# The last four blocks of each MLP written out as one list of single steps, and a raw buffer of its own for one down weight

## The chip, the cores and the metric

The kernel runs on one core of one Trainium2 chip. The time is the device time of one execution in microseconds (us); smaller is better. Below, the engines are called by the names of the profile: PE (TensorE, matrix products and transposes), ACT (ScalarE), DVE (VectorE), POOL (GpSimd) and SP (SyncE, whose queue issues the transfers; "SPq" in a timeline is the issue of one).

## The reference

The program is a small decoder trunk on 512 tokens of width 1024, in fp32: one layer with a pooling mixer, then one layer of stick-breaking attention (16 heads of 64), each followed by an MLP with a squared ReLU. Every mixer and MLP is framed by two RMS norms. Keys and values are projected once, from the residual stream after the first layer. Cut to what matters here:

```python
def sq_relu_mlp(h, w_up, w_down):
    u = jnp.matmul(h, w_up)                          # 512 x 4096
    return jnp.matmul(jnp.square(jax.nn.relu(u)), w_down)

for layer in range(2):
    h = rms_norm(x, mix_pre_g[layer])
    m = pool_mixer(h, ...) if layer < 1 else (stick_breaking_attention(...) @ w_o)
    x = x + rms_norm(m, mix_post_g[layer])
    h = rms_norm(x, mlp_pre_g[layer])
    x = x + rms_norm(sq_relu_mlp(h, w_up[layer], w_down[layer]), mlp_post_g[layer])
    if layer == 0:
        kv = rms_norm(x, kv_norm_g) @ w_kv
```

## The kernel before

**Tiling.** The 512 tokens are T = 4 tiles of 128; the residual stream is kept in `xt[0..3]`, each 128 tokens by 1024. The 4096 hidden units of an MLP are 32 blocks of 128. Each fp32 product is made of three products of a high and a low part (`mm3`, L284 to L286: high by high, high by low, low by high), so every weight and every activation is first split: the high part is a cast on ACT, the low part a subtract on DVE. For a weight this is `weight` (L142): a transfer into a tile "raw", of which there are two buffers (L144), the cast (L154) and the subtract (L156).

**An MLP** (`mlp`, from L604) works on a block of hidden units at a time: the up product (`up_block`, L705 to L707), ReLU (L619), square (L620), split. The down products of blocks 0 to 27 run in five groups, each as a scheme of seven products of half size (class `Seven`: products L587, sums into y on DVE L596, splits L265 and L266). The last four blocks, 28 to 31 (`plain` to `NJ`), are plain products: their down weights ("dn" in the rows) go through `weight`, their places come from `dn_pool`, and `contract` (L426) multiplies. In the last group `fill` (one new weight for each call, if there is a place for it) starts their loads.

**The finish of a tile** follows in `contract`. For each token tile, in two halves of 512 columns (in three cuts of 512, 256 and 256 for the last tile of the last layer): the products of four blocks on PE; `evacuate` on DVE, which adds the sums to y (L449); the sum of squares on ACT (L269); the product with the gain on DVE (L316); then `first_rstd`: the total on POOL (L273, for the three cuts L328) and the power to -1/2 (L280); `add_part` on DVE, which adds the normed result to x (L333). In layer 0 the squares of the new x follow (L269), a second total and power, the scale (`norm_part`, L371, ACT), eight transposes on PE (L385) and their split into the high part (`high`, L395 or L399 with a gain, ACT) and the low part (`low`, L404 or L408, DVE), which are the operands `xnh` and `xnl` of the next product: key and value (cast of a value L887). In layer 1 each cut is written out by SP (L346).

**What sets the order.** A scheduler orders each engine's instructions by a timeline of its own. Around `contract` only PE is held to the program's order (`manual_schedule(engines={PE})`); ACT, DVE and POOL are ordered by the scheduler. Each engine then works through its list in order. SP's queue is in order too: a transfer that waits for a buffer holds up those behind it.

**Key and value weights ahead.** During MLP 0 `split_apart` splits the weights of key, value and the like ahead of time: loads into tiles "apart" (three buffers), scale, cast and subtract in place, and then SP writes both parts to memory ("kept", L196); `make` (L226) reads them back when they are wanted ("w<-kept").

**MLP 1's beginning.** The attention's last steps end with a norm whose four high part copies (L399), scale (L371) and transposes (L385) lead into MLP 1's first up products; the weights of the first group of seven come by "w<-in_wdn" (L526).

Of the kernel before, what the change touches and what calls it, by code (L numbers as in the profile page):

```python
# [81 lines left out]
]  # L82


R_SCALE, R_MIX_POST0, R_MLP_PRE0, R_MLP_POST0, R_MIX_POST1, R_MLP_POST1 = range(6)

C_MIX_PRE0, C_KV, C_MIX_PRE1, C_MLP_PRE1 = range(4)
# [3 lines left out]
def trunk(ctx, tc, x, consts, grow, pw, wup, wdn, wq, wk, wv, wo, out):  # L91
    nc = tc.nc
# [46 lines left out]
    behind, latest = {}, {}  # L139


    def weight(src, tiles, scaled=None):  # L142
        raw = wts.tile([P, D], F32, tag="raw", bufs=2, name=name("raw"))
        nc.sync.dma_start(raw, src)  # L144

        def later(engine):
            return tc.issue_after(behind[engine].ins) if engine in behind else nullcontext()

        if scaled is not None:
            with later("pool"):  # L150
                scaled(raw)
        hi, lo = tiles
        with later("act"):
            nc.scalar.copy(hi, raw)  # L154
        with later("dve"):
            nc.vector.tensor_tensor(out=lo, in0=raw, in1=hi.bitcast(F32), op=ALU.subtract)  # L156
        return hi, lo
# [8 lines left out]

        return scaled

    gate, queue, made, ahead, dn_pool, att_pool = [False], [], {}, 4, [None], [None]

    def want(key, src, scaled=None):
        queue.append((key, src, scaled))
# [110 lines left out]
    def mm3(dst, ah, al, bh, bl, start, stop):  # L283
        nc.tensor.matmul(dst, ah, bh, start=start, stop=False)  # L284
        nc.tensor.matmul(dst, ah, bl, start=False, stop=False)  # L285
        nc.tensor.matmul(dst, al, bh, start=False, stop=stop)  # L286
# [9 lines left out]
    class Update:  # L296
# [18 lines left out]
            cut = self.cuts[n]  # L315
            nc.vector.tensor_tensor(out=self.scaled[:, cut], in0=y, in1=self.gpost[:, cut], op=ALU.mult)  # L316

        def square(self, n, y):

            self.squares_of(n, y)  # L320
            self.product(n, y)

        def first_rstd(self):
            if len(self.cuts) == 2:
                total(self.st, 0, self.eps)
# [15 lines left out]
        def add(self):  # L341
            self.first_rstd()
            for n, cut in enumerate(self.cuts):
                self.add_part(n)
                if self.final:
                    nc.sync.dma_start(out[TS[self.t], cut], xt[self.t][:, cut])  # L346
                else:
                    self.squares_of_x(n)

        def rstd(self):  # L350
            normed_by[self.t] = self
# [16 lines left out]
        def norm_part(self, n):  # L368
# [8 lines left out]
        def norm(self):  # L377
            for n in NS:
                self.norm_part(n)

        def transposes(self, h):
            pt = ps()
# [40 lines left out]
            if t in pending:  # L423
                pending.pop(t).transpose()

    def contract(lhs, w, y, first, update=None, tiles=range(T), soon=False):  # L426


        last = len(lhs) - 1
        ups = {}  # L430
        for t in tiles:
            up = ups[t] = update(t, y[t]) if update is not None else None
            cuts = up.cuts if up is not None else NS
            pds = [ps()[:, : cut.stop - cut.start] for cut in cuts]

            def product(n, cs):
                for c in cs:
                    (lh, ll), (wh, wl) = lhs[c], w[c]
                    mm3(
                        pds[n], lh[:, TS[t]], ll[:, TS[t]], wh[:, cuts[n]], wl[:, cuts[n]],  # L440
                        c == 0, c == last,
                    )

            def evacuate(n):
                part = y[t][:, cuts[n]]
                if first:
                    nc.scalar.copy(part, pds[n])
                else:
                    nc.vector.tensor_tensor(out=part, in0=pds[n], in1=part, op=ALU.add)  # L449
                if up is not None:  # L450
                    up.square(n, part)

            normed = up is not None and not up.final
            if t == 0:
                product(0, range(last))
                product(1, range(last))
                product(0, [last])
            else:
                product(0, range(last + 1))
            if normed and t == T - 1 and not soon:  # L460
                ups[0].transpose()
            evacuate(0)
            if normed and t > 0:
                ups[t - 1].rstd()
                ups[t - 1].norm()
            if t == 0:
                product(1, [last])
            elif normed and t == T - 1:
                product(1, [0])
                ups[1].transpose()  # L470
                product(1, range(1, last + 1))
            else:
                product(1, range(last + 1))
                if normed and soon and t == 2:
                    ups[0].transpose()
            evacuate(1)
            for n in range(2, len(cuts)):
                product(n, range(last + 1))
                evacuate(n)
            if up is None:  # L480
                fill()
            else:
                up.add()
                if normed and t == T - 2:
                    behind.update(latest)
        if normed:
            ups[T - 1].rstd()
            ups[T - 1].norm()
            for t in (T - 2, T - 1):
                pending[t] = ups[t]  # L490

# [106 lines left out]
    def mlp(l, mp, update):  # L598
# [57 lines left out]
        for g, group in enumerate(groups):  # L656
            coming = groups[g + 1] if g + 1 < len(groups) else None
            if coming:
                coming.squares()
            ups = list(range(firsts[g + 1], firsts[g + 1] + 2 * GROUPS[g + 1]) if coming else range(plain, NJ))  # L660
            if g == 0:
                up(ups.pop(0))
                fill()
            else:
                with tc.issue_after(latest["dve"].ins):
                    while entering:
                        entering.popitem()[1].homogeneous_eps()
            for i in range(7):
                group.product(i, y, written if g == 0 else None)
                if 7 * g + i in steps:  # L670
                    with tc.issue_after(latest["act"].ins), tc.issue_after(latest["dve"].ins):
                        split_apart(mp)
                if ups:
                    up(ups.pop(0))
                if i + 2 < 7:
                    group.make(i + 2)
                    if i + 2 == 4 and coming:
                        coming.load(0)
                    if i + 2 == 6 and coming:
# [11 lines left out]
                fill()  # L691
# [177 lines left out]
    with tc.tile_pool(name="att", bufs=1, reuse_waits="tile") as ap:  # L869
# [222 lines left out]
        def out_proj(u, tiles):  # L1092
            if u not in wos:
                wos[u] = [get(("o", 2 * u + c)) for c in range(2)]
            contract([os[2 * u + c] for c in range(2)], wos[u], y, u == 0, None, tiles)

        def end():

# [187 lines left out]
```

## Time and profile before

| | us |
|---|---|
| median of 3 runs | 956.77 (956.1 to 956.96) |
| span of the profiled execution | 955.0 |
| PE busy | 940.7 (98%) |
| DVE busy | 707.1 (74%) |
| ACT busy | 576.6 (60%) |
| POOL busy | 44.7 (5%) |
| last matmul starts | 946.71 |

The profile shows one execution, whose span of 955.0 us runs from its first to its last instruction; the median of the runs stands 1.8 us above it. Times in a timeline count from the start of the span. A row of a timeline gives start, length (both us), engine, line, operation, output<-input, sizes and, in brackets, how long the engine had been idle before and what ended that. Matmuls overlap, so a row's length is longer than the distance to the next one. A row "xN" holds N instructions in a row, and its length is that of all of them.

### The profile page before, as it was taken

How to read it: one execution, taken by the hardware profiler on the slowest of the kernel's cores; microseconds unless marked ns; L12 is line 12 of the kernel's file. 1: busy time of each engine (PE TensorE's matmuls, PEld its weight loads, DVE VectorE, ACT ScalarE, POOL GpSimd, SP SyncE). 2: the span in 40 equal slices, each digit the busy share in tenths (PEclk: the TensorE clock that was granted, in tenths of full speed). 3: DMA queues.
4: the chain of work that ended last, by engine and by line, in shares of the span. 5: the costliest groups of instructions: out<-in, count | busy, mean ns of one | idle time of the engine just before them, and what ended most of it. 6: DMA issues, size and time to landing. Idle time of an engine off the chain costs nothing.

```text
span 955.0 us, 12510 instructions
## 1 busy us (share of the span) xinstructions
PE 940.7 (98%) x4757; PEld 799.6 (84%) x4758; DVE 707.1 (74%) x810; ACT 576.6 (60%) x1015; POOL 44.7 (5%) x88
## 2 busy tenths in 40 slices
PE   9999999999999999999999999999999999999996
PEld 6998888888888878999899988898888888888885
DVE  5875799988979866476577778874595966957856
ACT  6667979788775646456656554775545544444632
POOL 2300000000000004000000000300000000000002
PEclk9999999999999999999999999999999999999998
DMA  8244969789697750422434271342513233133102
GB/s 307 99 175 151 338 216 359 293 282 343 221 326 266 273 192 2 179 88 88 162 125 171 95 265 45 127 139 68 197 39 129 97 132 110 45 132 110 47 21 88
DMA packets 43261, 156.14 MB, mean 163 GB/s; under 512 B 4289, under 2 KB 4673, under 8 KB 43202
## 3 DMA queue, kind: packets, MB, share of 16 engines
q1 hardware_dynamic: 43202, 155.36, 45.4%
q8 instruction: 37, 0.61, 0.3%
q14 instruction: 22, 0.18, 0.1%
HBM read 121.79 MB, written 33.55 MB: 163 GB/s over the span
## 4 chain that ended last, share of the span: by engine, by line
PE 86%; DVE 4%; ACT 3%; POOL 3%; DMA 2%; issue 1%; SPq 0%; POOLq 0%; DVEq 0%; ACTq 0%
PE ps L587 27%; PE ps L707 15%; PE ps L705 15%; PE ps L706 15%; PE ps L284 2%; PE ps L285 2%; PE ps L286 2%; PE ps L1040 2%; ACT xn L269 2%; PE ps L819 1%; PE ps L1023 1%; POOL stat L273 1%; DVE x L333 1%; PE ps L979 1%; POOL stat L280 1%
## 5 line engine op out<-in xcount | busy, mean ns | idle before, releaser
L587 PE MATMUL ps<-w,a 128*128 128x512 f32 x1176 | 278.6, 389 | 0.0
L707 PE MATMUL ps<-xnh,w 128*128 128x512 f32 (+1 forms) x712 | 261.6, 368 | 0.1
L706 PE MATMUL ps<-xnl,w 128*128 128x512 f32 (+1 forms) x712 | 261.5, 368 | 0.0
L705 PE MATMUL ps<-xnh,w 128*128 128x512 f32 (+1 forms) x712 | 261.2, 368 | 0.0
L587 PEld LDWEIGHTS ps<-w,a 128*128 128x128 f32 x1176 | 220.7, 188 | 45.9 <-DVE w L266 0.2
L707 PEld LDWEIGHTS ps<-xnh,w 128*128 128x128 f32 x712 | 134.2, 188 | 22.4 <-DVE w L840 0.3
L706 PEld LDWEIGHTS ps<-xnl,w 128*128 128x128 f32 x712 | 134.2, 189 | 21.8
L705 PEld LDWEIGHTS ps<-xnh,w 128*128 128x128 f32 x712 | 133.7, 189 | 22.1
L596 DVE TENSOR_TENSOR y<-ps,y 128x512 f32<-128x512 f32 x124 | 84.4, 686 | 42.0 <-PE ps L587 41.8
L156 DVE TENSOR_TENSOR w<-raw,w 128x1024 fp32r<-128x1024 f32 x58 | 70.9, 1222 | 57.7 <-ACT w L154 57.5
L154 ACT CAST w<-raw 128x1024 fp32r<-128x1024 f32 x58 | 61.0, 1051 | 80.5 <-PE ps L707 80.5
L265 ACT CAST a<-r 128x768 fp32r<-128x768 f32 (+1 forms) x60 | 47.6, 794 | 72.4 <-PE ps L587 54.6
L266 DVE TENSOR_TENSOR a<-r,a 128x768 fp32r<-128x768 f32 (+1 forms) x60 | 54.0, 900 | 11.8 <-ACT a L265 11.6
L265 ACT CAST w<-e 128x1536 fp32r<-128x1536 f32 (+1 forms) x30 | 41.8, 1395 | 25.6 <-DVE e L561 16.2
L1004 DVE TENSOR_TENSOR_SCAN e<-u,begin 128x1280 f32<-128x1280 f32 x16 | 45.2, 2822 | 11.3 <-ACT u L988 10.4
L266 DVE TENSOR_TENSOR w<-e,w 128x1536 fp32r<-128x1536 f32 (+1 forms) x30 | 49.4, 1647 | 1.8 <-ACT w L265 1.6
L165 ACT ACTIVATE apart<-apart,eye 128x128 f32<-128x128 f32 (+1 forms) x132 | 43.1, 407 | 0.2 <-DMA apart<-in_wk 0.2
L266 DVE TENSOR_TENSOR w<-w,w 128x1536 fp32r<-128x1536 f32 (+1 forms) x20 | 33.0, 1649 | 8.1 <-ACT w L265 8.1
L619 ACT ACTIVATE r<-ps 128x512 f32<-128x512 f32 x56 | 33.0, 589 | 8.3 <-PE ps L707 8.2
L284 PE MATMUL ps<-w,xnh 128*128 128x256 f32 x128 | 36.6, 286 | 1.4 <-ACT xnh L395 1.4
L266 DVE TENSOR_TENSOR w<-xn,w 128x1536 fp32r<-128x1536 f32 (+1 forms) x20 | 33.0, 1650 | 5.6 <-ACT w L265 5.5
L620 ACT ACTIVATE r<-r 128x512 f32<-128x512 f32 x56 | 35.5, 633 | 1.3
(131 smaller groups left out, 1394.7 us busy)
## 6 DMA issues: line engine op xcount, KB each, us to landing
raw<-in_wup SPq DMA_DIRECT2D x64, 512.0 KB, 3.8
w<-kept SPq DMA_DIRECT2D x60, 512.0 KB, 4.1
kept<-wx SPq DMA_DIRECT2D x30, 512.0 KB, 4.9
w<-in_wdn SPq DMA_DIRECT2D x8, 1536.0 KB, 7.7
kept<-apart SPq DMA_DIRECT2D x24, 512.0 KB, 5.1
xn<-in_wdn SPq DMA_DIRECT2D x8, 1536.0 KB, 8.2
raw<-in_wdn SPq DMA_DIRECT2D x8, 512.0 KB, 3.5
apart<-in_wk SPq DMA_DIRECT2D x7, 512.0 KB, 6.4
```

What stands on the lines that cost most here:

```text
L154: nc.scalar.copy(hi, raw)
L156: nc.vector.tensor_tensor(out=lo, in0=raw, in1=hi.bitcast(F32), op=ALU.subtract)
L165: nc.scalar.mul(c, c, gc[:, lo + k : lo + k + 1])
L265: latest["act"] = nc.scalar.copy(hi, src)
L266: latest["dve"] = nc.vector.tensor_tensor(out=lo, in0=src, in1=hi.bitcast(F32), op=ALU.subtract)
L284: nc.tensor.matmul(dst, ah, bh, start=start, stop=False)
L587: nc.tensor.matmul(bank, a[:, x, q, TS[t]], w[:, z, q], start=start and q == 0 and k == 0, stop=q == self.n - 1 and k == 2, skip_group_che ...
L596: nc.vector.tensor_tensor(out=part, in0=bank, in1=part, op=ALU.add)
L705: nc.tensor.matmul(pu[:, cols], wh[:, k, :], xnh[:, k, cols], start=k == 0, stop=False)
L706: nc.tensor.matmul(pu[:, cols], wh[:, k, :], xnl[:, k, cols], start=False, stop=False)
L707: nc.tensor.matmul(pu[:, cols], wl[:, k, :], xnh[:, k, cols], start=False, stop=k == KC - 1)
L1004: nc.vector.tensor_tensor_scan(out=self.e[:, ::-1], data0=self.u[:, 1:][:, ::-1], data1=begin[:, ::-1], initial=0.0, op0=ALU.mult, op1=ALU ...
```

## The change

1. `MLP_ORDER` lists, for each layer, single steps of the last four blocks. A new function `finish` runs the list, with the order of PE, ACT, DVE and POOL all held to it. The letters: p t n c..., products of tile t, cut n, blocks c; v evacuate; s squares; g product with the gain; V first rstd; a add to x; S squares of x; W second rstd; n norm part; t transposes; h and l high and low part; B marks what later weights may follow. `contract` keeps only the case without an update, which the output projection of the attention uses.
2. `weight` takes an optional `raw` tile. For block 30 (`NJ - 2`), the third of the four, the raw tile is a third buffer of the tag "apart", in place of one of the two "raw" buffers.
3. In the last step of the last group `fill` may start two weights instead of one.

In the program that results, the number of matmuls and of other operations is the same. In layer 0 PE's transposes of tile 0 stand ahead of the products of tile 3's first half, and those of tile 1 ahead of its second half; three matmuls of key and value change places; on ACT the second cast of a value (L887) stands ahead of both squares of the last tile's new x (step S30 and S31). Block 30's load stands in SP's queue behind a "kept<-apart" (the one issued at 319.68 before). In layer 1 its load stands right behind the "w<-in_wdn" issued at 607.03 before; its cast stands on ACT between the last squares (L269) and the four copies of L399 at the beginning of MLP 1, and its subtract on DVE between L1167 and L408.

```diff
+MLP_ORDER = [
+    last_steps("""p00012 p01012 p003 v00 s00 p013 v01 s01 g00 g01 V0 p100123 v10 s10 a00 S00 a01 S01 g10 W0
+    p110123 v11 s11 g11 V1 n00 n01 p200123 v20 s20 a10 S10 a11 S11 g20 W1 p210123 v21 s21 g21 V2 n10 n11
+    t00 t01 h00 h01 p300123 v30 s30 a20 a21 B t10 h10 S20 t11 h11 S21 W2 l00 l01 p310123 v31 s31 V3
+    l10 l11 g30 g31 n20 n21 a30 S30 a31 S31 W3 n30 n31"""),
+    last_steps("""p00012 p01012 p003 v00 s00 p013 v01 s01 g00 g01 V0 p100123 v10 s10 a00 a01 g10
+    p110123 v11 s11 g11 V1 p200123 v20 s20 a10 a11 g20 p210123 v21 s21 g21 V2 p300123 v30 s30 g30
+    p310123 v31 s31 a20 p320123 v32 s32 V3 a21 g31 g32 a30 a31 a32"""),
+]
...
-    def weight(src, tiles, scaled=None):
-        raw = wts.tile([P, D], F32, tag="raw", bufs=2, name=name("raw"))
+    def weight(src, tiles, scaled=None, raw=None):
+        if raw is None:
+            raw = wts.tile([P, D], F32, tag="raw", bufs=2, name=name("raw"))
...
-        made[k] = weight(src, place(k), scaled)
+        made[k] = weight(src, place(k), scaled, dn_raw.pop(k, None))
...
-    def contract(lhs, w, y, first, update=None, tiles=range(T), soon=False):
...
+    def contract(lhs, w, y, first, tiles):
...
+    def finish(l, lhs, w, y, update):
+
+        ups = [update(t, y[t]) for t in range(T)]
+        bank = {}
+
+        def product(t, n, *cs):
+            cut = ups[t].cuts[n]
+            if (t, n) not in bank:
+                bank[t, n] = ps()[:, : cut.stop - cut.start]
+            for c in cs:
+                (lh, ll), (wh, wl) = lhs[c], w[c]
+                mm3(
+                    bank[t, n], lh[:, TS[t]], ll[:, TS[t]], wh[:, cut], wl[:, cut], c == 0, c == len(lhs) - 1
+                )
...
+        on = mybir.EngineType
+        with tc.manual_schedule(engines={on.PE, on.Activation, on.DVE, on.Pool}):
+            for step, which in MLP_ORDER[l]:
+                steps[step](*which)
+        if l == 0:
             for t in (T - 2, T - 1):
                 pending[t] = ups[t]
...
                     c, d = (piece("apart", 1, 3)[:, 0] for _ in range(2))
+                    dn_raw["dn", l, NJ - 2] = mp.tile([P, D], F32, tag="apart", bufs=3, name=name("dn"))
...
-                fill()
+                fill(1 + (coming is None and i == 6))
...
-        with tc.manual_schedule(engines={mybir.EngineType.PE}):
-            contract(squares[1:], w, y, False, lambda t, y: update(t, y, gpost))
+        finish(l, squares[1:], w, y, lambda t, y: update(t, y, gpost))
```

More of the change, by code (lines that the diff above doesn't have):

```diff
@@ L82, with last_steps @@
 ]
+def last_steps(text):
+    return [(w[0], [int(c) for c in w[1:]]) for w in text.split()]
+MLP_ORDER = [
[7 more added lines that the diff above has]
+]
 R_SCALE, R_MIX_POST0, R_MLP_PRE0, R_MLP_POST0, R_MIX_POST1, R_MLP_POST1 = range(6)
@@ L167, in gains @@
         return scaled
-    gate, queue, made, ahead, dn_pool, att_pool = [False], [], {}, 4, [None], [None]
+    gate, queue, made, ahead, dn_pool, att_pool, dn_raw = [False], [], {}, 4, [None], [None], {}
     def want(key, src, scaled=None):
@@ L339, in squares_of_x @@
             square_sum(xt[self.t][:, cut], self.xn[:, cut], self.st, 4 + n)
[L341 to L348, printed above, removed]
         def rstd(self):
@@ L375, in norm_part @@
                 )
-        def norm(self):
-            for n in NS:
-                self.norm_part(n)
         def transposes(self, h):
@@ L424, in need @@
                 pending.pop(t).transpose()
-    def contract(lhs, w, y, first, update=None, tiles=range(T), soon=False):
+    def contract(lhs, w, y, first, tiles):
         last = len(lhs) - 1
-        ups = {}
         for t in tiles:
[L432 to L445, printed above, removed]
+            for n in NS:
+                pd = ps()
+                for c, ((lh, ll), (wh, wl)) in enumerate(zip(lhs, w)):
+                    mm3(pd, lh[:, TS[t]], ll[:, TS[t]], wh[:, n], wl[:, n], c == 0, c == last)
+                part = y[t][:, n]
@@ L446, in evacuate @@
                 if first:
-                    nc.scalar.copy(part, pds[n])
+                    nc.scalar.copy(part, pd)
                 else:
[L449 to L480, printed above, removed]
-                fill()
[L482 to L488, printed above, removed]
+                    nc.vector.tensor_tensor(out=part, in0=pd, in1=part, op=ALU.add)
+            fill()
@@ new lines, in finish, with evacuate, add, transposes @@
+    def finish(l, lhs, w, y, update):
[10 more added lines that the diff above has]
+                )
+        def evacuate(t, n):
+            part = y[t][:, ups[t].cuts[n]]
+            nc.vector.tensor_tensor(out=part, in0=bank.pop((t, n)), in1=part, op=ALU.add)
+        def add(t, n):
+            ups[t].add_part(n)
+            if l == 1:
+                cut = ups[t].cuts[n]
+                nc.sync.dma_start(out[TS[t], cut], xt[t][:, cut])
+        def transposes(t, h):
+            bank["t", t, h] = ups[t].transposes(h)
+        steps = {
+            "p": product, "v": evacuate, "a": add, "t": transposes, "B": lambda: behind.update(latest),
+            "s": lambda t, n: ups[t].squares_of(n, y[t][:, ups[t].cuts[n]]),
+            "g": lambda t, n: ups[t].product(n, y[t][:, ups[t].cuts[n]]),
+            "V": lambda t: ups[t].first_rstd(), "S": lambda t, n: ups[t].squares_of_x(n),
+            "W": lambda t: ups[t].rstd(), "n": lambda t, n: ups[t].norm_part(NS[n]),
+            "h": lambda t, h: ups[t].high(h, bank["t", t, h]), "l": lambda t, h: ups[t].low(h, bank["t", t, h]),
+        }
+        on = mybir.EngineType
[3 more added lines that the diff above has]
+        if l == 0:
@@ L1094, in out_proj @@
                 wos[u] = [get(("o", 2 * u + c)) for c in range(2)]
-            contract([os[2 * u + c] for c in range(2)], wos[u], y, u == 0, None, tiles)
+            contract([os[2 * u + c] for c in range(2)], wos[u], y, u == 0, tiles)
         def end():
```

4 lines of the change are left out of this document (removed).

## The prediction

> **What bounds the kernel now.** I read the page's busy shares first, then the chain of work that ended last, then the waits of TensorE alone, then the timeline around each wait that the change can reach.
>
> ```profile
> span 955.0 us, 12510 instructions
> PE 940.7 (98%) x4757; PEld 799.6 (84%) x4758; DVE 707.1 (74%) x810; ACT 576.6 (60%) x1015; POOL 44.7 (5%) x88
> PE 86%; DVE 4%; ACT 3%; POOL 3%; DMA 2%; issue 1%; SPq 0%; POOLq 0%; DVEq 0%; ACTq 0%
> 925.53 3.63 PE ps L587 x16
> ...
> PE ps L284 <- ACT xnh L395: 1.4, 1, 1.4
> PE ps L285 <- DVE dn L156: 0.8, 1, 0.8
> PE ps L284 <- ACT dn L154: 0.7, 1, 0.7
> ```
>
> TensorE is busy for 98% of the span, and the number of its matmuls stays as it is. One 512 column matmul follows the other every 3.63 / 16 = 0.227 us (fourth line, from the chain). So only two things can move the time: a wait of TensorE, or the stretch after its last matmul, where the chain leaves it. The three last lines (waits of TensorE: total, times, longest, us) name most of what the change can reach: one wait at the handover from MLP 0 to the key and value projection (xnh L395) and two for a down weight ("dn"). A fourth place, the transposes that begin MLP 1, is shown under C. Elsewhere TensorE runs back to back, and an edit there is worth nothing: the freed or added work of the other engines lies beside it.
>
> **The change, part by part.**
>
> A. Block 30's weight in layer 0. Timeline rows (start, length, engine, line, operation):
>
> ```profile
> 319.68 0.32 SPq L196 DMA_DIRECT2D kept<-apart  x1
> 334.54 0.51 SPq L196 DMA_DIRECT2D kept<-apart  x1
> 338.94 1.99 ACT L154 CAST dn<-raw 128x1024 fp32r<-128x1024 f32 x2
> 341.13 1.22 DVE L156 TENSOR_TENSOR dn<-raw,dn 128x1024 fp32r<-128x1024 f32 x1
> 342.38 2.06 SPq L144 DMA_DIRECT2D raw<-in_wdn  x2
> 342.87 1.22 DVE L156 TENSOR_TENSOR dn<-raw,dn 128x1024 fp32r<-128x1024 f32 x1
> 345.91 0.39 PE L286 MATMUL ps<-dn,sq 128*128 128x512 f32 x1
> 345.93 1.05 ACT L154 CAST dn<-raw 128x1024 fp32r<-128x1024 f32 x1 [5.00 <-DMA raw<-in_wdn]
> 347.03 0.50 PE L284 MATMUL ps<-dn,sq 128*128 128x512 f32 x1 [0.73 <-ACT dn L154]
> 348.29 0.50 PE L285 MATMUL ps<-dn,sq 128*128 128x512 f32 x1 [0.76 <-DVE dn L156]
> 348.85 0.40 PE L284 MATMUL ps<-dn,sq 128*128 128x512 f32 x1
> kept<-apart SPq DMA_DIRECT2D x24, 512.0 KB, 5.1
> ```
>
> Blocks 28 and 29 fill the two "raw" buffers. Block 30's load waits until the subtract at 341.13 + 1.22 = 342.35 has freed one, is issued at 342.38 and cast at 345.93, as soon as it has landed (3.55 later); and TensorE, which would have begun it at 345.91 + 0.227 = 346.14, begins at 347.03 (0.89 lost), gets the low part at 348.29 instead of 347.26 (1.03 more) and loses another 0.11 by the matmul at 348.85: 2.03.
>
> With a buffer of its own the load waits only for the write "kept<-apart" issued at 319.68, which empties that slot. By the median of 5.1 it lands at 324.8, the weight 3.55 later, by 328.4, well ahead of the cast, which now follows the two casts that end at 338.94 + 1.99 = 340.93. The subtract follows block 29's, which ends at 342.87 + 1.22 = 344.09, so it ends near 345.3, against a need at 346.14 + 0.227 = 346.37: 1.1 to spare. The two y adds (L596) that it pushes back only have to precede the adds of the finish, after this stage. One new wait comes: the low part goes into the slot that the last "kept<-apart" empties. This write is issued at 334.54 and by the median lands at 339.6; the subtract may start as late as 345.15, so the write would have to take 10.6 to be late. Block 31's load then goes out first at 342.38, lands at 345.9, is cast by 347.0 and subtracted by 348.2. TensorE wants its high part after twelve more matmuls (three of block 30, nine of the second half), at 346.14 + 12 x 0.227 = 348.86, and its low part at 349.09: no wait. Gain 2.03. Bounds: 0 (the late write takes it all) and 2.03 (no more is lost there); I take 2.03, as the spare is far above the median.
>
> B. The handover to key and value in layer 0:
>
> ```profile
> 376.03 0.28 PE L286 MATMUL ps<-w,xnl 128*128 128x256 f32 x1
> 376.98 0.63 ACT L269 ACTIVATE xn<-x 128x512 f32<-128x512 f32 x1 [3.12 <-DVE x L333]
> 377.61 0.35 ACT L887 CAST v<-ps 128x256 fp32r<-128x256 f32 x1
> 378.68 0.30 POOL L273 TENSOR_SCALAR stat<-stat 128x1 f32<-128x1 f32 x1 [2.58 <-ACT xn L269]
> 379.66 1.33 ACT L371 ACTIVATE xn<-x,stat 128x512 f32<-128x512 f32 x2 [1.07 <-POOL stat L280]
> 380.90 1.05 ACT L395 CAST xnh<-ps 128x512 fp32r<-128x512 f32 x2
> 381.51 0.39 PE L284 MATMUL ps<-w,xnh 128*128 128x256 f32 x1 [1.45 <-ACT xnh L395]
> ```
>
> TensorE waits 1.45 for tile 2's high part (380.90), which stands on ScalarE behind tile 3's norm: squares of its x (376.98 and, behind the cast of v, 377.86), their sum on GpSimd 378.68, the scale 379.66. If everything were only shifted by A it would start at 379.48. In the listed order the cast of v (L887) stands ahead of both squares on ScalarE, and needs TensorE's second value product, whose last matmul starts at 376.03 before, hence 374.00 after A and, as three value and key matmuls change places, near 374.1, ending at 374.40. Squares at 374.72 and 375.35, sum 376.25 (0.82 behind the second square, as in the rows), scale 377.24, high part 378.48, TensorE 379.09. That is 2.42 ahead of 381.51: 0.39 beyond A. Ends: 0 (only A's shift) and 1.45 (the whole wait goes); I take 0.39, which is a sum of rows. The transposes of tiles 0 and 1, moved ahead of tile 3's products, and the squares, products and scales that change places cost nothing: TensorE's products of tile 3 cover them.
>
> C. The start of MLP 1. There the load of block 30 now comes first in ScalarE's and VectorE's queues, ahead of tile 2's high parts (L399) and tile 3's scale:
>
> ```profile
> 611.45 0.39 PE L286 MATMUL ps<-w,ohl 128*128 128x512 f32 x1
> 621.85 1.11 ACT L399 ACTIVATE xnh<-ps,eye 128x128 fp32r<-128x128 f32 x4
> 623.79 1.27 PE L385 MATMUL ps<-eye,xn 128*128 128x128 f32 x8 [0.37 <-ACT xn L371]
> w<-in_wdn SPq DMA_DIRECT2D x8, 1536.0 KB, 7.7
> ```
>
> The slot's last reader is the matmul at 611.45, so the load goes out near 611.9. By 3.55 it lands at 615.5; by 7.7, the slowest kind of load near it, at 619.6. At 621.85 it is there, and its cast (1.05 in the row of 345.93, 0.95 to 1.05 from one to the next) goes first. The four copies of L399 start at 622.8, the scale behind them as much later, the transposes at 624.6 to 624.7 instead of 623.79. TensorE has no further wait in MLP 1 that could give this back: plus 0.85 (0.82 to 0.95). The subtract lies beside this on VectorE. In exchange a cast and a subtract disappear from the last group of MLP 1, where they hid behind TensorE: nothing.
>
> D. The end. Rows of the last tile:
>
> ```profile
> 943.63 0.69 DVE L316 TENSOR_TENSOR y<-y,grow 128x512 f32<-128x512 f32 x1 [0.79 <-ACT xn L269]
> 943.71 0.87 POOL L273 TENSOR_SCALAR stat<-stat,eps 128x1 f32<-128x1 f32 x1 [3.52 <-ACT xn L269]
> 945.25 1.42 DVE L333 SCALAR_TENSOR_TENSOR x<-y,stat,x 128x512 f32<-128x512 f32 x2 [0.92 <-POOL stat L280]
> 946.71 0.28 PE L286 MATMUL ps<-dn,sq 128*128 128x256 f32 x1
> 947.51 1.02 DVE L316 TENSOR_TENSOR xn<-y,grow 128x512 f32<-128x512 f32 x2
> 948.45 0.42 DVE L449 TENSOR_TENSOR y<-ps,y 128x256 f32<-128x256 f32 x1
> 949.56 0.19 POOL L328 TENSOR_TENSOR stat<-stat 128x1 f32<-128x1 f32 x1 [0.59 <-ACT xn L269]
> 950.42 1.54 DVE L333 SCALAR_TENSOR_TENSOR x<-xn,stat,x 128x512 f32<-128x512 f32 x3 [1.09 <-POOL stat L280]
> L273 POOL TENSOR_SCALAR stat<-stat x24: 294/300/2186, 5.0 to 622.0; 128x1 f32<-128x1 f32 x24
> L273 POOL TENSOR_SCALAR stat<-stat,eps x8: 375/864/869, 354.1 to 948.6; 128x1 f32<-128x1 f32 x8
> ```
>
> The last products end at 946.71 + 0.28 = 946.99, but the last evacuation (L449) starts only at 948.45: VectorE has the two adds of tile 2 (945.25), two evacuations and two products (947.51) ahead of it. In the list the evacuations of tile 3 stand ahead of tile 2's adds and the products g31 and g32 behind the last evacuation. It can start at 947.02, 1.43 earlier. Its square, the sum L328 and the add at 950.42 follow it by 950.42 - 948.45 = 1.97 before, so the add would start near 949.0: a gain of 1.42. But the products now run on VectorE from 948.0 to 948.85, exactly when GpSimd would take L328 (948.14). The two first rows show what such a neighbour does: tile 2's sum starts 0.08 behind an L316 product and takes 0.87. The two last rows (shortest, median, longest in ns) hold all such sums: those with the operand eps, which are taken beside products, have a median of 864, the others of 300, with 2186 once. Then L328 ends behind the products, near 949.0, its power takes it on, and the add starts at 949.69: a gain of 0.73. Ends 0 and 1.42; I take 0.73, since the row at 943.71, with the same neighbour, shows the hold. From the add to the end of the span nothing changes.
>
> This one the Trainium skill speaks against too: its page "SBUF — State Buffer", section "Who interferes with whom", says that VectorE and GpSimd share a port pair that one of them locks, so that the loser is blocked for the whole instruction. The trace agrees, by 864 against 300; by the page the gain would be 0.73, without it 1.42.
>
> The sum: -2.03 - 0.39 + 0.85 - 0.73 = -2.30, so a span of 955.0 - 2.3 = 952.7. The median of the runs shown, 956.77, stands 1.74 above this span; with the same distance it comes to 954.5. A measurement of this kernel can tell about 0.2%, or 1.9, from no change, so the forecast lies just outside.
>
> **The rivals.**
>
> 1. GpSimd isn't held at the end, because L328 comes a little ahead of the products: -2.30 - 0.69 = -2.99, 953.8. For it speaks the small distance, 0.14; against it the row at 943.71, whose product also began first, by only 0.08.
>
> 2. The layer 0 wait is only replaced. Block 30's subtract needs the last "kept<-apart" to have landed; each us that it lands after 345.15 costs a us. At 346.5, 12.0 instead of 5.1, it takes back 1.35: 955.9, within 0.2%. The same comes if VectorE reaches the subtract later than its rows say. That the change doesn't do what it says, because SyncE's queue still holds the load back until 342, would end at the same place; against it, the two rows of SPq at 319.68 and 334.54 show that the queue moves on in that time.
>
> 3. Slower: ScalarE stands at the start of MLP 1 for a weight that has not landed. Its queue is in order, so tile 2's high parts and tile 3's scale wait behind the cast. Each us of landing after 621.85 costs a us: with -2.30 as a base it ends over 0.2% slower once the load lands after 621.85 + 2.30 + 1.91 = 626.1, 14.2 after its issue. At 627.5 it gives 954.5 + 5.65 = 960.1. For it: this is the only place where a load of the far future is put ahead of work that TensorE waits for at once. Against: 7.7 is the longest median there.
>
> **How the numbers follow.** The forecast with A to D as summed gets 0.47, rival 1 0.15, rival 2 and smaller gains of any kind 0.24, rival 3 and its like 0.14. So faster by over 0.2% has 0.62, within 0.2% 0.24, slower 0.14. Predicted is 954.5. The range goes from 953.4 (the other end of D and 0.4 of what B could still give) to 956.6 (all of A lost and no more): it leaves out most of rival 3 and a little below. The forecast's own range is 953.8 to 955.2.
>
> **What would show it.** A: no wait of TensorE on dn L154 or L156 in layer 0, and the load of block 30 issued between 322 and 325. B: a wait for xnh L395 of some 1.2 instead of 1.45, the first key and value matmul after it near 379.1. C: a cast dn L154 near 621.9 and the transposes 0.85 later relative to the matmul at 611.45. D: L449's last start 0.3 behind the last product, and L328 longer than 0.19. A wait for a DMA on ScalarE at C, a "kept<-apart" landing behind 344 or new waits of TensorE in the finish would prove the forecast wrong.

## The result

The changed kernel takes 954.3 us (median of 7 runs, 953.63 to 954.42), the kernel before 956.77 beside it (956.1 to 957.52). The ratio is 0.9973, with a 95% interval of 0.9962 to 0.9984: faster by about 0.27%. The medians differ by 2.47 us, against 2.30 forecast (954.5). The span of the profiled execution is 951.9 against 955.0. Of these 3.2 us, 0.66 lie ahead of everything that the change touches (the first product with a down weight in layer 0 starts at 340.49 instead of 341.15) and are chance: in the executions below that start lies anywhere from 340.49 to 341.34.

**The profile after.** The page's span, busy shares and chain by engine, then the waits of TensorE (total, times, longest, us). Line numbers have moved: L154 is L170 now, L156 L172, L269 L285, L273 L289, L280 L296, L284 to L286 are L300 to L302, L316 L332, L328 L339, L333 L344, L371 L373, L385 L383, L395 L393, L399 L397, L449 L455.

```profile
span 951.9 us, 12511 instructions
PE 940.5 (99%) x4758; PEld 799.6 (84%) x4758; DVE 707.5 (74%) x810; ACT 576.9 (61%) x1015; POOL 45.5 (5%) x88
PE 93%; ACT 2%; POOL 1%; DVE 1%; issue 1%; DMA 1%; SPq 0%; POOLq 0%; DVEq 0%; ACTq 0%
...
PE ps L383 <- ACT xn L373: 1.3, 2, 1.1
PE ps L300 <- ACT xnh L393: 0.9, 1, 0.9
```

Both waits for "dn" are gone. The wait for xnh has shrunk from 1.4 to 0.9, and the one of the transposes for xn has grown from 0.5 to 1.3. TensorE does the same work (940.5 against 940.7).

A, timeline of layer 0 (start, length, engine, line, operation):

```profile
319.04 0.32 SPq L212 DMA_DIRECT2D kept<-apart  x1
321.66 0.33 SPq L160 DMA_DIRECT2D dn<-in_wdn  x1
340.18 1.05 ACT L170 CAST dn<-dn 128x1024 fp32r<-128x1024 f32 x1
341.72 0.33 SPq L160 DMA_DIRECT2D raw<-in_wdn  x1
343.34 1.22 DVE L172 TENSOR_TENSOR dn<-dn,dn 128x1024 fp32r<-128x1024 f32 x1
345.25 0.39 PE L302 MATMUL ps<-dn,sq 128*128 128x512 f32 x1
345.48 0.39 PE L300 MATMUL ps<-dn,sq 128*128 128x512 f32 x1
345.32 1.05 ACT L170 CAST dn<-raw 128x1024 fp32r<-128x1024 f32 x1 [4.10 <-DMA raw<-in_wdn]
```

Block 30's load (dn<-in_wdn) goes out at 321.66, 20 us ahead of its old place (each taken from the first product with a down weight), its cast and its subtract (343.34, ended 344.56) are done well ahead of the matmul at 345.48, and TensorE goes on in its 0.23 pitch from 345.25. The load at 341.72 is now block 31's.

B, the handover to key and value:

```profile
373.74 0.37 ACT L877 CAST v<-ps 128x256 fp32r<-128x256 f32 x1 [0.57 <-PE ps L302]
374.01 0.64 ACT L285 ACTIVATE xn<-x 128x512 f32<-128x512 f32 x1
375.44 0.30 POOL L289 TENSOR_SCALAR stat<-stat 128x1 f32<-128x1 f32 x1 [2.50 <-ACT xn L285]
376.42 1.33 ACT L373 ACTIVATE xn<-x,stat 128x512 f32<-128x512 f32 x2 [1.07 <-POOL stat L296]
377.66 1.05 ACT L393 CAST xnh<-ps 128x512 fp32r<-128x512 f32 x2
378.28 0.38 PE L300 MATMUL ps<-w,xnh 128*128 128x256 f32 x1 [0.94 <-ACT xnh L393]
```

The cast of v stands ahead of the squares and sets their start, as forecast, and the rest of the chain keeps its old distances.

C, the start of MLP 1:

```profile
608.68 0.33 SPq L160 DMA_DIRECT2D dn<-in_wdn  x1
618.65 1.03 ACT L170 CAST dn<-dn 128x1024 fp32r<-128x1024 f32 x1
619.59 1.12 ACT L397 ACTIVATE xnh<-ps,eye 128x128 fp32r<-128x128 f32 x4
620.60 1.33 ACT L373 ACTIVATE xn<-x,stat 128x512 f32<-128x512 f32 x2
621.37 0.94 PE L383 MATMUL ps<-eye,xn 128*128 128x128 f32 x5 [1.14 <-ACT xn L373]
```

The cast goes first. Counted from tile 2's transposes, it pushes the four copies back by 0.93 against before, and the scale and tile 3's transposes by 0.78 and 0.77; it waits for no transfer (its row has no releaser), since the load left 10 us ahead of it.

D, the end:

```profile
944.60 0.42 DVE L455 TENSOR_TENSOR y<-ps,y 128x256 f32<-128x256 f32 x1 [0.35 <-PE ps L302]
944.94 0.74 DVE L344 SCALAR_TENSOR_TENSOR x<-y,stat,x 128x512 f32<-128x512 f32 x1
945.60 0.75 DVE L332 TENSOR_TENSOR xn<-y,grow 128x256 f32<-128x256 f32 x2
945.72 0.35 POOL L339 TENSOR_TENSOR stat<-stat 128x1 f32<-128x1 f32 x1 [1.05 <-ACT xn L285]
946.14 0.63 POOL L296 TENSOR_TENSOR stat<-stat,mhalf 128x1 f32<-128x1 f32 x1
946.81 0.75 DVE L344 SCALAR_TENSOR_TENSOR x<-xn,stat,x 128x512 f32<-128x512 f32 x1 [0.45 <-POOL stat L296]
```

The last evacuation waits for TensorE alone, 0.32 behind the last matmul's start at 944.28. GpSimd's last sum takes 0.35 beside a product and 0.19 before.

**The span cut in pieces.** To compare executions that start differently, each span is cut at the same instructions: the first and the last matmul with a down weight in layer 0 (A lies between), the matmul that follows tile 2's transposes (B), tile 3's transposes in MLP 1 (C), the last matmul, the last tile's first add (D) and the end. Each piece is the difference of two starts in the trace of that kernel, in us; the kernels below the second are those of the experiments.

| kernel | start | A | B | C | to last matmul | D | add to end | span | SP records |
|---|---|---|---|---|---|---|---|---|---|
| before | 341.15 | 29.02 | 11.34 | 242.28 | 322.92 | 3.71 | 4.61 | 955.03 | 466 |
| changed | 340.49 | 26.95 | 10.84 | 243.09 | 322.91 | 2.53 | 5.04 | 951.85 | 468 |
| changed, again | 341.02 | 27.22 | 10.83 | 243.05 | 322.92 | 2.52 | 5.05 | 952.61 | 468 |
| order only | 341.18 | 29.15 | 10.83 | 242.28 | 322.92 | 2.52 | 4.62 | 953.50 | 466 |
| raw buffer only | 341.34 | 27.32 | 11.34 | 243.05 | 322.91 | 3.71 | 5.05 | 954.72 | 468 |
| raw buffer in layer 0 only | 341.03 | 27.00 | 10.84 | 242.27 | 322.91 | 2.53 | 5.02 | 951.60 | 467 |
| before, one more transfer | 340.83 | 29.01 | 11.37 | 242.28 | 322.93 | 3.72 | 4.99 | 955.13 | 468 |
| layer 0 only, tile 0 out in one | 340.96 | 26.99 | 10.84 | 242.29 | 322.92 | 2.52 | 4.84 | 951.36 | 465 |
| layer 0 only, tiles 0 and 1 out in one each | 341.07 | 26.98 | 10.83 | 242.28 | 322.93 | 2.52 | 4.73 | 951.34 | 463 |
| no product beside the last sum | 341.11 | 27.00 | 10.83 | 243.05 | 322.91 | 2.30 | 5.05 | 952.25 | 468 |
| g30 last | 340.94 | 27.41 | 10.84 | 243.05 | 322.92 | 2.53 | 5.05 | 952.74 | 468 |

From before to changed: A -2.07, B -0.50, C +0.81, D -1.18, the stretch behind the add +0.43. Together -2.51, and the medians differ by 2.47. The columns "add to end" and "SP records" (SyncE's records in the trace) hold what the prediction did not see.

### The profile page after: what moved, and what is told of

It is laid out like the page before. It is cut to its first block, busy times and chain, and to the rows that moved or that the text cites. A ratio compares the mean times of both kernels' runs of the same rounds, so it can differ in the third digit from the quotient of the medians.

```text
span 951.9 us, 12511 instructions
## 1 busy us (share of the span) xinstructions
PE 940.5 (99%) x4758; PEld 799.6 (84%) x4758; DVE 707.5 (74%) x810; ACT 576.9 (61%) x1015; POOL 45.5 (5%) x88
## 4 chain that ended last, share of the span: by engine, by line
PE 93%; ACT 2%; POOL 1%; DVE 1%; issue 1%; DMA 1%; SPq 0%; POOLq 0%; DVEq 0%; ACTq 0%
PE ps L577 28%; PE ps L697 15%; PE ps L695 15%; PE ps L696 15%; PE ps L300 4%; PE ps L302 4%; PE ps L301 4%; PE ps L1030 2%; PE ps L1013 2%; PE ps L809 1%; PE ps L969 1%; ACT xn L285 1%; PE ps L970 1%; PE ps L383 1%; POOL stat L289 1%
## 5 line engine op out<-in xcount | busy, mean ns | idle before, releaser
L172 DVE TENSOR_TENSOR w<-raw,w 128x1024 fp32r<-128x1024 f32 x58 | 70.9, 1222 | 56.7 <-ACT w L170 56.5
L170 ACT CAST w<-raw 128x1024 fp32r<-128x1024 f32 x58 | 61.0, 1051 | 78.0 <-PE ps L697 77.8
L300 PE MATMUL ps<-w,xnh 128*128 128x256 f32 x128 | 36.5, 286 | 0.9 <-ACT xnh L393 0.9
```

## The experiments

**The parts apart.** Three kernels and the changed one again, timed beside the kernel before on one chip. The first keeps the list and drops the raw buffer:

```diff
-                    dn_raw["dn", l, NJ - 2] = mp.tile([P, D], F32, tag="apart", bufs=3, name=name("dn"))
-                fill(1 + (coming is None and i == 6))
+                fill()
```

> The listed order alone; block 30's weight goes through the two shared raw buffers again, in both layers. Theory (the four terms are separate): the layer 0 wait for the weight is back (two waits of TensorE on dn L170 and L172, about 2.0 together), the 0.8 at the start of MLP 1 is gone, B (about -0.5) and D (about -1.2) stay. Sum about -1.7 against before, near 955.1. Rival (the order gains only because the products run without a gap): the wait eats B too, since tile 3's norm chain then stands where it stood, and about -1.2 is left, near 955.6.

Measured: 955.35 against 956.85, ratio 0.9984 (0.9975 to 0.9993). The waits of TensorE in its trace:

```profile
PE ps L300 <- ACT xnh L393: 0.9, 1, 0.9
PE ps L300 <- ACT dn L170: 0.9, 1, 0.9
PE ps L301 <- DVE dn L172: 0.8, 1, 0.8
PE ps L383 <- ACT xn L373: 0.5, 2, 0.4
```

The two waits for dn are back in full, the transposes wait 0.5 as before, and the wait for xnh stays at 0.9. By the pieces A and C are those of before (+0.13, 0.00), B and D those of the changed kernel (-0.51, -1.19): -1.56, measured -1.50. So B is the list's own gain and does not hang on the raw buffer; the rival falls. That it is the place of the cast of v within the list is read from the chain in B; the single swaps of the list were not run apart.

The second is the kernel before with the raw buffer and without the list:

```diff
+        if raw is None:
+            raw = wts.tile([P, D], F32, tag="raw", bufs=2, name=name("raw"))
...
+                    dn_raw["dn", l, NJ - 2] = mp.tile([P, D], F32, tag="apart", bufs=3, name=name("dn"))
...
+                fill(1 + (coming is None and i == 6))
```

> Before, with only the raw buffer of its own and the second load in the last step; ACT, DVE and POOL ordered by the scheduler as before. Theory: -2.0 from the layer 0 wait, +0.8 at the start of MLP 1 (the cast stands there too), end unchanged (last evacuation 1.4 to 1.5 behind TensorE): about -1.2, near 955.6. Rival (the freed wait only moves into the handover to key and value, which this order does not shorten): TensorE's wait for xnh there grows by up to 2.0, and the time is that of before or up to 0.8 above it, 956.8 to 957.6.

Measured: 956.21 against 956.85, ratio 0.9985 (0.9976 to 0.9994). The medians differ by 0.64, the interval holds 0.6 to 2.3.

```profile
PE ps L285 <- ACT xnh L396: 1.4, 1, 1.4
...
PE ps L386 <- ACT xn L372: 1.3, 2, 1.1
```

The wait for xnh is 1.4 as before, not 2.0 longer: the time that A frees isn't lost at the handover. The transposes' wait is 1.3, so C comes with the raw buffer, with or without the list. The pieces give A -1.70, C +0.77 and, against the expectation of an unchanged end, +0.44 behind the add: -0.49.

The third has the raw buffer in layer 0 alone:

```diff
-                    dn_raw["dn", l, NJ - 2] = mp.tile([P, D], F32, tag="apart", bufs=3, name=name("dn"))
+                    if l == 0:
+                        dn_raw["dn", l, NJ - 2] = mp.tile([P, D], F32, tag="apart", bufs=3, name=name("dn"))
...
-                fill(1 + (coming is None and i == 6))
+                fill(1 + (l == 0 and coming is None and i == 6))
```

> The changed kernel, with the raw buffer of its own in layer 0 only; in layer 1 block 30's cast goes back to the end of MLP 1. Theory: the transposes at the start of MLP 1 come 0.8 earlier again and nothing later takes it back: 0.8 below the changed kernel, near 953.5, and about -3.3 against before. Rival (the cast at the end of MLP 1 now meets the listed order and delays the first products there, or the transposes wait for something else): the time of the changed kernel, 954.3, with a wait of TensorE on dn in layer 1 of about 0.8.

Measured: 953.41 against 956.85, ratio 0.9955 (0.9943 to 0.9967), and 0.98 below the changed kernel's 954.39 in the same comparison (in the two traces 0.78 of it is C and 0.22 is A). Timeline rows of this kernel:

```profile
619.20 1.11 ACT L397 ACTIVATE xnh<-ps,eye 128x128 fp32r<-128x128 f32 x4
621.14 0.55 PE L383 MATMUL ps<-eye,xn 128*128 128x128 f32 x3 [0.38 <-ACT xn L373]
...
918.38 1.05 ACT L170 CAST dn<-raw 128x1024 fp32r<-128x1024 f32 x1 [1.86 <-PE ps L577]
```

The copies follow the squares with no cast between, the transposes wait 0.38 instead of 1.14, and the cast runs at 918.38, beside TensorE's last group, where nobody waits for it. C is 242.27, that of before. The expectation holds, the rival falls. In layer 1 the buffer removes no wait and costs the 0.8.

The changed kernel again:

> The changed kernel again, beside the others: about -2.5 against before. The first executions of the two kernels differ by 0.64 before anything of the change is reached and by 0.48 behind the last add. If both are chance, other executions show other values there, and the difference of the medians is the sum of the four terms, -2.9; if the 0.48 belongs to the change, it is there again and the difference is -2.5.

Measured: 954.39 against 956.85, ratio 0.9963 (0.995 to 0.9975). The two differences that the expectation names are 0.66 and 0.43 in the table above. The start is 341.02 now: that difference was chance. The stretch behind the add is 5.05 again: that one was not. A is 0.27 longer than in the first execution. Rows of TensorE and ScalarE there:

```profile
346.68 1.05 ACT L170 CAST dn<-raw 128x1024 fp32r<-128x1024 f32 x1 [4.92 <-DMA raw<-in_wdn]
...
348.73 0.39 PE L300 MATMUL ps<-dn,sq 128*128 128x512 f32 x1
349.04 0.50 PE L301 MATMUL ps<-dn,sq 128*128 128x512 f32 x1
349.38 0.40 PE L302 MATMUL ps<-dn,sq 128*128 128x512 f32 x1
```

Block 31's weight was cast 0.83 later than in the first execution (346.68 - 341.02 against 345.32 - 340.49), because its transfer landed later, and TensorE waited 0.09 and 0.11 for its low part. That is what is late next. In the six kernels of the experiments with this buffer in layer 0 the loss at this place is 0 in four, 0.24 with the raw buffer only and 0.40 with g30 last.

**The end of the span.** With the raw buffer, 0.4 is lost where no work of the kernel is left. The transfers of the core in the stretch from the last tile's first add to the end, of the changed kernel (from 946.8):

```profile
q1 hardware_dynamic: 529, 0.69, 38.1%
q14 instruction: 1, 0.01, 0.7%
```

and of the kernel with the order only (from 948.9):

```profile
q1 hardware_dynamic: 523, 0.68, 41.3%
```

(packets, MB, share of the DMA engines). A packet of an instruction queue falls into the stretch in the one and not in the other. The close of the program on SyncE is a row of waits for the outputs, then a drain, a second drain, a semaphore event, a third drain and a last event. The three drains (shortest, median, longest in ns), of the changed kernel and of the one with the order only:

```profile
L1272 SPq DRAIN x3: 7/7/129, 951.0 to 951.4; - x3
...
L1271 SPq DRAIN x3: 7/7/23, 952.7 to 953.3; - x3
```

In the changed kernel the first drain starts at 950.96 and takes 0.13, 0.34 behind the instruction ahead of it; with the order only it takes 0.007 and follows at 0.04. The packet comes some 0.6 behind the late drain (near 951.6). The raw buffer gives SyncE two more waits (468 records of it in the trace instead of 466). Two kernels change that count by other means. The first splits an early output of the kernel before:

```diff
+                if self.final and self.t == 0 and n == 0:
+                    for q in (slice(0, 256), slice(256, 512)):
+                        nc.sync.dma_start(out[TS[0], q], xt[0][:, q])
-                if self.final:
+                elif self.final:
                     nc.sync.dma_start(out[TS[self.t], cut], xt[self.t][:, cut])
```

> Before, with the first half of token tile 0 written out in two transfers instead of one, far ahead of the end: SyncE's program gets two instructions longer, as the raw buffer makes it (468 of SyncE's records instead of 466). Theory (the 0.43 behind the last add is the fetch of one more piece of SyncE's program): from the last tile's first add to the end of the span 5.0 instead of 4.6, with an instruction transfer in that stretch, and the time up by 0.4, 957.2. Rival (the 0.43 comes from the raw buffer itself, the place of its load or its tile): 4.6, no transfer, 956.8.

Measured: 4.99 behind the add, with one packet of the same instruction queue in it. The time is 957.3 against 957.05, ratio 1.0003 (0.9994 to 1.0012): the 0.4 is below what the runs resolve, the trace shows it. So it doesn't need the raw buffer. The second takes two instructions away from the kernel with the raw buffer in layer 0:

```diff
-            if l == 1:
-                cut = ups[t].cuts[n]
+            if l == 1 and (t or n):
+                cut = ups[t].cuts[n] if t else slice(0, D)
```

> The changed kernel with the raw buffer in layer 0 only, and token tile 0 written out by one transfer instead of two: SyncE's program gets two instructions shorter, 465 records. Theory (fetch): from the last tile's first add to the end 4.6 instead of 5.0, no instruction transfer there, and 0.4 below the kernel with the raw buffer in layer 0 only: about 953.0, and about -3.8 against before. Rival (the raw buffer itself): 5.0, and 953.4.

Measured: 953.31 against 957.05, ratio 0.9963 (0.9949 to 0.9976); 4.84 behind the add. Half of the expectation: the first two drains take 0.007, but now the third, at 951.03, takes 0.13 and comes 0.36 behind the instruction ahead of it. The packet comes near 951.7, again some 0.6 behind the late drain and 0.3 behind the end of the span. The point had moved on with the count instead of away. A last kernel moves it two further, by writing tile 1 out in one transfer too:

```diff
-            if l == 1 and (t or n):
-                cut = ups[t].cuts[n] if t else slice(0, D)
+            if l == 1 and (t > 1 or n):
+                cut = ups[t].cuts[n] if t > 1 else slice(0, D)
```

> The changed kernel with the raw buffer in layer 0 only, and token tiles 0 and 1 each written out by one transfer instead of two: SyncE's program is four instructions shorter, 463 records. Theory (a piece of SyncE's program is fetched at a fixed count of its instructions, and with 468, 467 and 465 records this point falls on the first, the second and the third drain of the close): with 463 it falls behind the last drain, the stretch from the last tile's first add to the end takes 4.6, and the time is 0.4 below the kernel with the raw buffer in layer 0 only, near 953.0. Rival (the fetch only moves on and always costs something): 4.8 to 5.0, 953.2 to 953.4.

Measured: 953.12 against 956.86, ratio 0.9961 (0.9947 to 0.9975); all drains take 0.007, and 4.73 is left. With 468, 467 and 465 records the late instruction is the first, the second and the third drain, and the stretch takes 5.04, 5.02 and 4.84. With 466 and 463 no drain is late, the packet comes only behind the end of the span (by 0.3 in the kernel before, 0.6 with the order only, 1.0 with 463), and the stretch takes 4.61 and 4.73. But 466 has its late instruction too: the semaphore event between the second and the third drain starts 0.36 behind the second drain (order only, at 953.16) instead of 0.15. It costs nothing, since GpSimd is still at its own part of the close until 953.26 and SyncE's third drain stands at 953.26 too. So the late place moves by one instruction for each record, and what it costs hangs on what the other engines are doing then. From SyncE's last wait for an output to the end, the close takes 1.25, 1.24, 0.82, 1.00 and 0.83 with 468, 467, 466, 465 and 463 records. That this instruction waits for a piece of the program is inferred from the packet behind it; no row shows the wait itself. The 0.12 by which the last kernel's stretch is longer than that of the kernel before lies ahead of the close: SyncE's last wait for an output comes 3.91 behind the add instead of 3.79. Its time is the lowest of all kernels run, but within the runs' scatter it is the same as 953.31 and 953.41.

**GpSimd beside a product.** Two kernels, each run once, try the end. In the first the two last products are taken out of the way. It leaves out the part of blocks 28 to 31 in them, so its rows count here and not its time:

```diff
-    p210123 v21 s21 g21 V2 p300123 v30 s30 g30
-    p310123 v31 s31 a20 p320123 v32 s32 V3 a21 g31 g32 a30 a31 a32
+    p210123 v21 s21 g21 V2 g31 g32 p300123 v30 s30 g30
+    p310123 v31 s31 a20 p320123 v32 s32 V3 a21 a30 a31 a32
```

> The changed kernel; the two products with the gain of the last two cuts (g31, g32) are taken ahead of the last tile's products, on sums that are not complete, so that VectorE has none of them beside GpSimd's last sum. Left out is the part of blocks 28 to 31 in those products. Theory (GpSimd is held by the product beside it): L339 takes 0.19 instead of 0.35, the power 0.56 instead of 0.63, and the last tile's first add stands 0.23 to 0.25 closer to the last matmul: 2.30 instead of 2.53. Rival (the 1.43 of VectorE's earlier evacuation is lost elsewhere, on ScalarE or in the semaphores): 2.53 stays.

Timeline of GpSimd there:

```profile
946.33 0.19 POOL L339 TENSOR_TENSOR stat<-stat 128x1 f32<-128x1 f32 x1 [1.04 <-ACT xn L285]
946.60 0.56 POOL L296 TENSOR_TENSOR stat<-stat,mhalf 128x1 f32<-128x1 f32 x1
```

Both take their short times, and D is 2.30: the contact with g31 and g32 costs the changed kernel 0.23, as expected, and without it D would have gained 1.41, the forecast's outer end of 1.42. The second kernel, with 954.51 in its one run, puts a 512 wide product last:

```diff
-    p210123 v21 s21 g21 V2 p300123 v30 s30 g30
-    p310123 v31 s31 a20 p320123 v32 s32 V3 a21 g31 g32 a30 a31 a32
+    p210123 v21 s21 g21 V2 p300123 v30 s30 a20
+    p310123 v31 s31 a21 g31 p320123 v32 s32 V3 g32 g30 a30 a31 a32
```

> The changed kernel; in the last tile the adds of tile 2 stand ahead of the evacuations, and behind the last evacuation stand g32 and then g30, which is 512 wide, where the changed kernel has the second add of tile 2, g31 and g32. Theory (GpSimd waits for the end of the one instruction that began before its own, and gets in between two): L339 begins in the middle of g30 and waits for its end, 0.35 to 0.5 long, the last tile's first add 2.5 to 2.7 behind the last matmul. Rival (it waits until VectorE has none left): since g30 is the last, the same; but then the power isn't held at all, 0.56, and the changed kernel's power of 0.63 has to come from g32, which ran on behind it.

```profile
945.94 1.02 DVE L332 TENSOR_TENSOR xn<-y,grow 128x256 f32<-128x256 f32 x2
946.59 0.42 POOL L339 TENSOR_TENSOR stat<-stat 128x1 f32<-128x1 f32 x1 [0.88 <-ACT xn L285]
947.09 0.56 POOL L296 TENSOR_TENSOR stat<-stat,mhalf 128x1 f32<-128x1 f32 x1
```

The sum starts within g30, the second of the two instructions, takes 0.42 and ends at 947.01, 0.05 behind g30's end at 946.96; with nothing behind it the power takes 0.56. In the changed kernel the sum ends at 946.07, 0.05 behind the end of g31 at 946.02, while g32 runs on to 946.35, and the power beside g32 takes 0.63. So in both the sum waits for the one product that was running when it began, and in the changed kernel it gets in ahead of the end of the next. D is 2.53 in both: putting the wide product last neither gains nor loses.

## Why the prediction was right, and where it wasn't

The forecast case came about: 954.5 was said, 954.3 measured, within the range, and the sign and the size (-2.30 against -2.47) hold. Term by term:

- **A, -2.03 forecast, -2.07 in the first execution, -1.6 to -2.0 in the others.** The step holds: load and cast early, no wait of TensorE for block 30. The spare of block 30's subtract was smaller than reckoned (see rival 2 below). "No wait" for block 31 was too good: its transfer sets the time next and lands up to 0.4 too late in some executions.
- **B, -0.39 forecast, -0.50 measured.** The chain through the second cast of v is the one in the trace; the forecast's sums were 0.1 long. Of that, 0.08 is a slip: 0.82 behind a second square at 375.35 is 376.17, not 376.25. Order alone has it, so the shift by A and the gain of B add up as said.
- **C, +0.85 forecast, +0.81 measured.** Undoing the buffer in layer 1 takes exactly this away and nothing gives it back.
- **D, -0.73 forecast, -1.18 measured.** This is the term that was mis-sized. The step that failed is "Then L328 ends behind the products": the sum is held by one product, the one that runs when it begins, for 0.16, and the power beside the next for 0.07, not by both products for 0.69. The row taken as the pattern, the sum at 943.71 of before, is another operation (a TENSOR_SCALAR) and stood beside a single 512 wide product that had just begun, so it could not show what a second product does; the one of the changed kernel began 0.1 into a 256 wide product. The truth lay between forecast and rival 1, nearer to the rival.
- **"From the add to the end of the span nothing changes": wrong, +0.43.** SyncE's program became two instructions longer, and one of its drains now comes 0.3 late where SyncE is on the path. That it was nearly made up by D's extra 0.45 is luck.

Of the rivals, the late "kept<-apart" of rival 2 cost nothing, but it came close. In the first execution the subtract of block 30 started at 343.34, straight behind block 29's. In four of the other seven executions with the buffer in layer 0 it waited for that write, longest with the raw buffer only:

```profile
345.11 1.23 DVE L157 TENSOR_TENSOR dn<-dn,dn 128x1024 fp32r<-128x1024 f32 x1 [0.84 <-DMA kept<-apart]
```

There the subtract ended 0.25 ahead of the matmul that needs it (346.59). The last write took 7.6 to 10.3 in these eight executions, not the median of 5.1 by which the prediction called the spare large, and 0.25 to 1.2 was left. In the second execution of the changed kernel it landed at 344.49, behind the 344 that the prediction names as a sign of being wrong, and A held all the same. ScalarE did not wait for a transfer at C: load to cast is 10 us. Rival 1's mechanism, GpSimd not held, is refuted in part: it is held, but briefly. What the third edit, the second `fill` in the last step, does by itself is not shown: no run has the raw buffer without it.

The Trainium skill's rule weighed in the prediction ("SBUF — State Buffer", "Who interferes with whom") is borne out in its kind: with the products out of the way the sum takes 0.19 and the power 0.56, beside them 0.35 and 0.63. The page's "fully blocks" stands there for VectorE's two-port modes; of an instruction with two inputs in SBUF, as these products are, it says that it contends with a GpSimd instruction that reads SBUF. A sum that ends 0.05 behind the product's end, in two orders, fits a block for that whole instruction; adding up all products in the queue was this forecast's own reading, not the page's.

## What to carry to other kernels

When a buffer is given to a late load, look where the same edit lands in every other stage that shares the code: here layer 0 gained 2.0 and layer 1 lost 0.8, and making the edit in layer 0 alone gave 953.41 against 954.39. A short GpSimd operation that begins beside one of VectorE's products is held: here the sum was held by what was left of the one product that was running, in two orders. The row of 2.19 in the kernel before goes the other way, so price such a meeting both ways. When a step leans on a transfer's median, look at that very transfer's own time: this write took up to 10.3 where the median was 5.1. Where a tenth of a per cent is at stake, the close of the program counts too, and so does the number of instructions of the engine that closes it.

## What was not expected of the hardware

Two more instructions in SyncE's program, far ahead of the end, made the close longer by 0.4 us: a drain there came late, with a packet of an instruction queue behind it. With 468, 467, 466, 465 and 463 records of SyncE the stretch behind the last add took 5.04, 5.02, 4.61, 4.84 and 4.73, and from 468 to 465 the late instruction was the next one of the close with each record fewer. And GpSimd's small sum, beside two products in a row, ended 0.05 behind the end of the first. The row of 2.19 in the kernel before (GpSimd, L273, from 615.56) stays unexplained by that: there VectorE had three instructions in a row, from 615.17 to 617.59, and the sum ended behind the third, at 617.75. That was not tried.
